# Adding the residual in one-tile transfers, with a larger descriptor room and other buffer addresses, in a hybrid conv/RWKV decoder layer

## The chip, the cores and the metric

The kernel runs on one core of a Trainium2 chip. A core has TensorE (PE, matmuls into PSUM), VectorE (DVE), ScalarE (ACT), GpSimd (POOL), and SyncE (SP), which here only issues transfers between DRAM and the on-chip SBUF; sixteen DMA engines carry them. GpSimd issues transfers too, through a queue of its own whose descriptors stand in a piece of SBUF that the program sets aside. The metric is device microseconds for the whole layer, median of several runs; lower is better.

## What is computed

One decoder layer over 512 positions and 16 learned meta tokens ahead of them, model width 2048, all float32:

```python
n = rmsnorm(h, g_pre_mix)
z = n @ w_in                                   # 2048 -> 6592 columns
y_conv = short_conv_group(z[..., :CONV_COLS], conv_w)
y_rwkv = rwkv7_group(z[..., CONV_COLS:], ...)  # token shift, low-rank gates, a scan over 16 heads of 64
mix = jnp.concatenate([y_conv, y_rwkv], axis=-1) @ w_out
h = h + rmsnorm(mix, g_post_mix)               # the residual addition that the change touches
f = conv_glu(rmsnorm(h, g_pre_ffn), w_gate_up, conv_ffn, w_down)   # 2048 -> 2 x 5632 -> 2048
h = h + rmsnorm(f, g_post_ffn)
```

## The kernel before

Activations lie transposed: 16 k tiles of 128 channels (partitions) by positions. Every large product is made of three float32r products of a rounded part and a remainder (hi·hi, hi·lo, lo·hi): ScalarE rounds (`S.copy`, or an activation with a scale), VectorE subtracts to get the remainder. For weights, a raw tile of 512 KB comes into one of five buffers R; `parted` (L1313) rounds it into H or another tile and puts the remainder in O or another tile.

The first stage (about 0 to 760 us) computes the input projection, the RWKV scan and the convolution group. Its pool of tiles, p1, is given back and a second pool, p2, takes the memory. Then `w_out` is multiplied, into `acc` (in this part called `h`), for two halves of the positions: columns 0 to 257 (half 0) and 258 to 513 (half 1).

Then comes the part around the change. `rms1(i)` (L1245) makes the reciprocal root `r1[i]` of half i from the sums of squares. `residual(i)` (L1271) goes through the k tiles in eight pairs: VectorE multiplies the pair by `r1`, GpSimd issues a transfer that reads the layer's input `xT` from DRAM and adds it into the tile in SBUF (`accum_op=ALU.add`), and then `split` scales, rounds and takes the remainder of each of the two tiles: these are the moving operands of the feed-forward's first products, `tt` (block `b11`) for k tiles 0 to 7 of half 0, and `ahi`/`alo` for the others. In half 1 SyncE also stores the pair, 512 KB, to DRAM (`hsp`), and ScalarE and VectorE square and sum the tiles for the next norm (`beside`, L1547).

TensorE meanwhile runs `halves2` (L1530) for the first two column blocks of the feed-forward, f = 0 and f = 1: all of half 0 for both, then half 1. Each k tile of a half feeds 12 matmuls of 128x128 by 256 or 258 columns: gate and up of two blocks, three products each. f = 2 and 3 follow, and then a long, regular stretch of sevenfold products to the end.

Everything up to the first units of that stretch is recorded first and put in order by a planner (class `Plan`): `run` (L423) lets a model of the five engines walk through the recorded work, with a cost for each instruction (`time`, 0.9 us for a GpSimd transfer) and a time of landing (`land`, L330: bytes at 230 GB/s, one transfer behind the other, and a fixed part), eight times with new ranks; the best order is written out, and every engine executes its list in that order. A late transfer therefore also holds up whatever stands behind its reader.

GpSimd's issues stand in its list one after the other, with one square sum of the norm among the first. A helper records every operation, so that nearly all instructions of the profile carry its line, L223; tiles tell them apart.

Of the kernel before, what the change touches and what calls it, by code (L numbers as in the profile page):

```python
# [10 lines left out]
F32 = mybir.dt.float32  # L11
F32R = mybir.dt.float32r
AF = mybir.ActivationFunctionType
ALU = mybir.AluOpType
# [8 lines left out]
KT = D // 128  # L23
CW = 1024
NP = 8
# [3 lines left out]
T0 = META - 2  # L29
TY = L - T0  # L30
# [9 lines left out]
COLS = {}  # L40
NCOL = 0
# [50 lines left out]

FILL = 9

TRIES = 8
LAND, GAP = 1.2, {"PE": 0.3, "DVE": 0, "ACT": 0, "POOL": 0, "SP": 0}

# [25 lines left out]
class View:  # L123
# [57 lines left out]
        return self.then("unsqueeze", (d,), {}, self.parts, np.expand_dims(self.ids, d))  # L181

    def to_broadcast(self, shape):
        return self.then("to_broadcast", (shape,), {}, self.parts, self.ids)

    def bitcast(self, dtype):
        return self.then("bitcast", (dtype,), {}, self.parts, self.ids)
# [39 lines left out]
class Plan:  # L227
# [195 lines left out]
    def run(self, rank):  # L423

        units, cost = self.units, self.cost
        left, ready = [len(b) for b in self.before], [0.0] * len(units)
        wait, go = {e: [] for e in HOP}, {e: [] for e in HOP}
        free, busy = dict.fromkeys(HOP, 0.0), dict.fromkeys(HOP, (0.0, False))
        free["PE"] = self.head
        self.pipe, table, kind = 0.0, 0, (128, 128)  # L430
        began, ends = [0.0] * len(units), [0.0] * len(units)
        for u in range(len(units)):
            if not left[u]:
                heapq.heappush(wait[self.engine[u]], (0.0, u))
        for _ in units:
            t, e = min((free[e] if go[e] else max(free[e], wait[e][0][0]), i, e) for i, e in enumerate(HOP)
                       if go[e] or wait[e])[::2]
            while wait[e] and wait[e][0][0] <= t:
                u = heapq.heappop(wait[e])[1]
                heapq.heappush(go[e], (rank[u], u))  # L440
            u = heapq.heappop(go[e])[1]
            x = units[u][0]
            start = t
            if e in ("DVE", "POOL") and self.two(x):
                end, two = busy["POOL" if e == "DVE" else "DVE"]
                if two and end > t:

                    aside = [u]
                    while e == "DVE" and go[e] and self.two(units[aside[-1]][0]):
                        aside.append(heapq.heappop(go[e])[1])  # L450
                    u = aside.pop() if not self.two(units[aside[-1]][0]) else aside.pop(0)
                    for v in aside:
                        heapq.heappush(go[e], (rank[v], v))
                    x = units[u][0]
                    if self.two(x):
                        start = end
            d = cost[u]
            if e == "ACT":
                k = self.TABLE.get(x["kw"].get("func"), 0)
                if k and k != table:  # L460
                    d, table = d + 1.28, k
            if e == "PE":
                k = self.mode(x)
                if k != kind:
                    d, kind = d + (0.25 if k == (128, 128) else 0.1), k
            began[u], ends[u] = t, start + d
            free[e], busy[e] = start + d, (start + d, self.two(x))
            dma = x["op"] == "dma_start"
            end = self.land(x, start + d) if dma else start + d + (0.22 if e == "PE" else 0)
            for v in self.after[u]:  # L470
                o = self.engine[v]
                ready[v] = max(ready[v], start + d if o == e and not dma else end + 0.07 + GAP[o])
                left[v] -= 1
                if not left[v]:
                    heapq.heappush(wait[o], (ready[v], v))
        return began, ends
# [13 lines left out]
def hymba(tc, I, out, ysp=None):  # L490
    nc = tc.nc
# [6 lines left out]
    def pool(ctx, name, bufs, kind="sbuf"):  # L498
        kw = {} if kind == "sbuf" else {"space": PSUM if kind == "psum" else DRAM}
        return Pool(plan, ctx.enter_context(tc.tile_pool(name=name, bufs=bufs, **kw)), bufs, kind)  # L500

    cp, ap, wp = pool(ctx, "cp", 1), pool(ctx, "ap", 1), pool(ctx, "wp", 2)
    mp, dp = pool(ctx, "mp", 2, "psum"), pool(ctx, "dp", 1, "dram")
    plan.on = True

    par = cp.tile([128, NCOL], F32, name="par")
    SP.dma_start(par[:, :KT], I["par"][:, :KT])
    ones = cp.tile([128, 128], F32, name="ones")
    z0 = cp.tile([128, 1], F32, name="z0")
    V.memset(z0, 0.0)  # L510
    S.activation(out=z0, in_=z0, func=AF.Copy, scale=1.0)
    omu = cp.tile([128, 28 + NP], F32, name="omu")

    def pc(n, i):
        return par[:, COLS[n] + i:COLS[n] + i + 1]

    if ysp is None:
        ysp = dp.tile([KT, 128, TY], F32, name="ysp")
# [64 lines left out]
    def rms(ss, r, m, q, psp, tag, pb=2, eps=None, o=None):  # L583


        n = r.shape[-1]
        ps = psp.tile([128, 512], F32, name="psn", tag=tag, bufs=pb)[:, :n]
        for i, x in enumerate(ss):
            PE.matmul(ps, ones, x, start=(i == 0), stop=(i == len(ss) - 1))
        if eps is None:  # L590
            V.tensor_scalar(out=m, in0=ps, scalar1=1.0 / D, scalar2=EPS, op0=ALU.mult, op1=ALU.add)
        else:
            V.scalar_tensor_tensor(out=m, in0=ps, scalar=1.0 / D, in1=eps, op0=ALU.mult, op1=ALU.add)
        rsqrt_guess(m, r, q)
        V.tensor_scalar(out=q, in0=q, scalar1=-0.5, scalar2=1.5, op0=ALU.mult, op1=ALU.add)
        V.tensor_tensor(out=r if o is None else o, in0=r, in1=q, op=ALU.mult)
# [4 lines left out]

    with ExitStack() as ctx1:
        p1, aux, stp = pool(ctx1, "p1", 1), pool(ctx1, "aux", 2, "psum"), pool(ctx1, "st", 2, "psum")
        cst = p1.tile([128, 64 + 9 * C], F32, name="cst")
        gmask = cst[:, :64]
        smask = cst[:, 64:]
        SUV = []
        for i in range(3):
            t = p1.tile([128, 2, 2, 64], F32, name=f"SUV{i}")
# [9 lines left out]
        for k in range(KT):  # L619
            xr = p1.tile([128, LP], F32, name="krv"[k % 3], bufs=2)[:, :L]  # L620
            SP.dma_start(xr, I["xT"][k])
            if k == 1:
                SP.dma_start(par[:, KT:], I["par"][:, KT:])
                V.tensor_scalar(out=omu[:, :28], in0=par[:, COLS["mu"]:COLS["mu"] + 28], scalar1=-1.0, scalar2=1.0,
                                op0=ALU.mult, op1=ALU.add)
                V.tensor_scalar(out=omu[:, 28:], in0=par[:, COLS["k_a"]:COLS["k_a"] + NP], scalar1=-1.0, scalar2=1.0,
                                op0=ALU.mult, op1=ALU.add)
            if k == 2:
                SP.dma_start(ones, I["cst"][:, :128])
                SP.dma_start(cst, I["cst"][:, 256:])  # L630
            if k == 0:
                first = wload(I["w_in"][0][0])
            hi, lo = a_tiles(k, L)
            split(xr, hi, lo, pc("g_pre", k))
            xs.append((hi, lo))
            sq = p1.tile([128, LP], F32, name=("sg", "al", "t1", "t2", "t3", "Pi")[k if k < 2 else 2 + k % 4])[:, :L]
            S.activation(out=sq, in_=xr, func=AF.Square)
            if k < 2:
                ss.append(sq)
            else:  # L640
                (G, V)[k % 2].tensor_tensor(out=ss[k % 2], in0=ss[k % 2], in1=sq, op=ALU.add)
# [576 lines left out]
    with ExitStack() as ctx2:  # L1218
# [16 lines left out]
        def big(tag, dtype=F32R):  # L1235
            return p2.tile([128, 1024], dtype, name=tag, bufs=WB[tag])
# [34 lines left out]
        def residual(i):  # L1271

            a, b = HY[i]
            c, d = WIN[i]
            for m in range(0, KT, 2):
                x, src = h[:, m:m + 2, a:b], I["xT"][m:m + 2, :, T0 + a:T0 + b].rearrange("m p t -> p m t")
                V.tensor_tensor(out=x, in0=x, in1=r1[i].unsqueeze(1).to_broadcast([128, 2, b - a]), op=ALU.mult)
                G.dma_start(x, src, accum_op=ALU.add)
                for n in (m, m + 1):
                    with plan.step(1):  # L1280
                        split(h[:, n, c:d], *act(n, i), pc("g_ffn", n))
                if i:
                    SP.dma_start(hsp[m:m + 2].rearrange("m p t -> p m t"), h[:, m:m + 2, 2:])
                yield
# [46 lines left out]

        def sums(j):

            y = [big("R", F32)[:, :TY] for _ in range(2)]
            for x, k in zip(y, (j, H + j)):
                SP.dma_start(x, ysp[KORD[k]])
            t = two()
            less(t[:, 0], y[1][:, 256:], y[0][:, 256:])
            plus(t[:, 1], t[:, 0], y[0][:, :258])
            x = y[1][:, :258]  # L1340
            less(x, x, t[:, 1])
            for o, x in ((T2, t[:, 1]), (T3, t[:, 0]), (T4, x)):
                split(x, o[:, j, 0], o[:, j, 1])
# [660 lines left out]
```

## Time and profile before

| | |
|---|---|
| median of 3 runs | 2448.86 us (2447.86 to 2452.65) |
| the profiled execution | 2448.97 us, span 2447.2 us |
| TensorE busy | 2375.2 us, 97% of the span |
| VectorE, ScalarE, GpSimd busy | 1755.9, 1228.2, 647.5 us |
| mean DMA rate | 113 GB/s |
| mean granted TensorE clock | 0.985 |

Three stretches are not full of matmuls: the first microseconds, where the first tiles are loaded; about 960 to 1062 us, the part described above; and the last 28 us. A row of the timeline has the start, the time, the engine, the operation with its output and inputs, a count, and in brackets the idle time before it with what ended it. "issue" there means that the profile shows no wait that the engine had. A group's row has its total and mean time, and the idle time before its members.

### The profile page before, as it was taken

To read this page: it belongs to the slowest core of one execution; us is meant where nothing else is said; L and a number is where in the kernel's file an instruction comes from. 1 tells how busy PE (TensorE), PEld (TensorE's weight loads), DVE (VectorE), ACT (ScalarE), POOL (GpSimd) and SP (SyncE) were. 2 spreads that over 40 slices of the span, in tenths; PEclk is the share of its full clock that TensorE was granted. 3 is DMA by queue.
4 is the path that set the end of the run, shared out by engine and by line. 5 is a ranking of instruction groups with operands and counts; after the bars stand their busy time and mean duration, and the time that the engine had idled before them with its cause. 6 is when DMAs were issued, how large, how long until landed. Compare 5 with 4: busy or idle time off the path is not lost.

```text
span 2447.2 us, 46249 instructions
## 1 busy us (share of the span) xinstructions
PE 2375.2 (97%) x18450; PEld 2253.0 (92%) x18450; DVE 1755.9 (72%) x2361; ACT 1228.2 (50%) x2404; POOL 647.5 (26%) x742
## 2 busy tenths in 40 slices
PE   7999999999999999599999999999999999999996
PEld 7999999999999999499999999898989898989896
DVE  7678888879745776267676767686868585959586
ACT  7766766767654555265443434342435252525254
POOL 2222646465450022201121212121212020202025
PEclk9999999999999999699999999999999999999998
DMA  5444333333434745533232324242424242323352
GB/s 179 150 130 118 93 84 92 105 105 94 127 105 132 231 136 178 107 94 97 85 121 79 121 78 129 69 131 69 134 74 130 78 120 85 111 91 102 98 193 71
DMA packets 136295, 276.82 MB, mean 113 GB/s; under 512 B 30576, under 2 KB 47728, under 8 KB 136080
## 3 DMA queue, kind: packets, MB, share of 16 engines
q1 hardware_dynamic: 131728, 269.66, 36.1%
q0 software_dynamic: 4352, 4.21, 1.3%
q8 instruction: 145, 2.38, 0.4%
q14 instruction: 70, 0.57, 0.1%
HBM read 247.99 MB, written 25.84 MB: 112 GB/s over the span
## 4 chain that ended last, share of the span: by engine, by line
PE 89%; issue 3%; DVE 3%; DMA 2%; ACT 2%; POOL 1%; SPq 0%; ACTq 0%; POOLq 0%; DVEq 0%
PE mps L223 56%; PE u L223 17%; PE d L223 10%; PE st L223 4%; PE aux L223 2%; DVE acc L223 1%; POOL acc L223 1%; DMA acc<-xT_dram 0%; DMA R<-w_down_dram 0%; DMA l<-lo 0%; DVE raw L223 0%; DMA k<-xT_dram 0%; DMA d<-tb 0%; DVE O L223 0%; DVE alo L223 0%
## 5 line engine op out<-in xcount | busy, mean ns | idle before, releaser
L223 ACT CAST H<-R 128x1024 fp32r<-128x1024 f32 x401 | 419.2, 1047 | 492.7 <-PE u L223 187.0
L223 DVE TENSOR_TENSOR O<-R,H 128x1024 fp32r<-128x1024 f32 x401 | 521.9, 1302 | 126.6 <-ACT H L223 119.5
L223 PE MATMUL mps<-ahi,whi 128*128 128x264 f32 (+2 forms) x1824 | 365.1, 289 | 10.6 <-ACT whi L223 10.6
L223 PE MATMUL mps<-alo,whi 128*128 128x264 f32 (+2 forms) x1824 | 364.3, 289 | 0.9 <-DVE alo L223 0.9
L223 PE MATMUL mps<-ahi,wlo 128*128 128x264 f32 (+2 forms) x1824 | 361.5, 288 | 1.6 <-DVE wlo L223 1.6
L223 PE MATMUL mps<-tt,H 128*128 128x258 f32 x2160 | 290.2, 284 | 7.5 <-ACT tt L223 6.2
L223 PEld LDWEIGHTS mps<-ahi,whi 128*128 128x128 f32 x1824 | 278.6, 189 | 13.2 <-ACT whi L223 10.8
L223 PE MATMUL mps<-ahi,H 128*128 128x258 f32 x1064 | 262.8, 287 | 25.9 <-ACT ahi L223 25.5
L223 PEld LDWEIGHTS mps<-tt,H 128*128 128x128 f32 x2160 | 273.5, 190 | 10.5 <-ACT tt L223 7.2
L223 DVE TENSOR_TENSOR wlo<-raw,whi 128x512 fp32r<-128x512 f32 x261 | 198.6, 765 | 117.8 <-ACT whi L223 102.4
L223 PEld LDWEIGHTS mps<-alo,whi 128*128 128x128 f32 x1824 | 278.0, 189 | 3.5 <-DVE alo L223 1.1
L223 PEld LDWEIGHTS mps<-ahi,wlo 128*128 128x128 f32 x1824 | 277.5, 190 | 3.8 <-DVE wlo L223 1.8
L223 POOL TENSOR_TENSOR raw<-raw,rb 128x516 f32<-128x516 f32 (+1 forms) x45 | 91.5, 2034 | 677.0 <-DVE raw L223 628.0
L223 PE MATMUL mps<-alo,H 128*128 128x258 f32 x1064 | 263.1, 287 | 0.4
L223 POOL TENSOR_TENSOR R<-R 128x1024 f32<-128x1024 f32 x40 | 131.7, 3292 | 429.6 <-DVE R L223 429.6
L223 DVE TENSOR_TENSOR R<-R 128x1024 f32<-128x1024 f32 x136 | 227.7, 1674 | 1.6 <-DMA R<-w_pair_dram 0.3
L223 PEld LDWEIGHTS mps<-ahi,H 128*128 128x128 f32 x1064 | 200.4, 191 | 28.9 <-ACT ahi L223 28.4
L223 ACT CAST whi<-raw 128x512 fp32r<-128x512 f32 x261 | 160.2, 618 | 119.0 <-PE mps L223 74.0
L223 PEld LDWEIGHTS mps<-alo,H 128*128 128x128 f32 x1064 | 201.8, 193 | 2.9 <-DVE alo L223 2.9
L223 POOL TENSOR_SCALAR SUV<-VT 32x64 f32<-32x64 f32 x272 | 138.7, 510 | 159.6 <-PE st L223 132.8
L223 PE MATMUL mps<-ahi,O 128*128 128x258 f32 x1064 | 159.9, 286 | 0.0
L223 PE MATMUL mps<-tt,O 128*128 128x258 f32 x1080 | 153.6, 281 | 0.0
(323 smaller groups left out, 4603.6 us busy)
## 6 DMA issues: line engine op xcount, KB each, us to landing
R<-w_gu_dram SPq DMA_DIRECT2D x176, 512.0 KB, 3.6
raw<-w_in_dram SPq DMA_DIRECT2D x208, 256.0 KB, 2.7
R<-w_down_dram SPq DMA_DIRECT2D x88, 512.0 KB, 3.7
raw<-w_out_dram SPq DMA_DIRECT2D x32, 256.0 KB, 4.4
R<-w_pair_dram SPq DMA_DIRECT2D x16, 512.0 KB, 4.5
l<-lo SPq DMA_DIRECT2D x24, 264.0 KB, 2.3
R<-ysp SPq DMA_DIRECT2D x16, 257.0 KB, 4.3
hsp<-acc SPq DMA_DIRECT2D x8, 512.0 KB, 2.8
```

The source lines that it names most:

```text
L223: return getattr(self.real, op)(*real, **{k: x.get() if isinstance(x, View) else x for k, x in kw.items()})
```

## The change

- The room for GpSimd's descriptors goes from 1024 to 2048 bytes per partition (`DGE`).
- `residual` issues a transfer for each k tile, two for a pair, where it issued one; the product on VectorE and the stores stay in pairs.
- The planner gets a list `ring` of GpSimd's transfers in flight: one of 128 partitions counts 2 + 128 // 8 = 18 entries, `DGE // 16` = 128 entries are there, and a transfer that finds no room waits for the earliest landing.
- The room comes out of SBUF: `ones` becomes one column, set by VectorE and read as a repeated column (it was loaded, 64 KB), and the parameters are kept in two tiles, of which the one for the first stage, and `omu`, lie in p1. `to_broadcast` now also repeats the numbers by which dependences are found.
- In `sums` the two rows for j = 0 go to H and O instead of two R buffers. The pool places tiles in the order of their first use, so H and O now lie at 150784 to 175359 bytes of each partition (before: 200416 to 224991), and the three blocks `tt` behind them (175360 to 224895; before 150880 to 200415). Most other tiles move by 96 bytes.

```diff
+DGE = 2048
...
+                n = 2 + x["out"].parts // 8
+                while sum(k for t, k in ring if t > start) + n > DGE // 16:
+                    start = min(t for t, _ in ring if t > start)
...
-            end = self.land(x, start + d) if dma else start + d + (0.22 if e == "PE" else 0)
+            if dma and e == "POOL":
+                ring.append((self.land(x, start + d), n))
+            end = ring[-1][0] if dma and e == "POOL" else self.land(x, start + d) if dma else start + d + (0.22 if e == "PE" else 0)
...
-    par = cp.tile([128, NCOL], F32, name="par")
-    SP.dma_start(par[:, :KT], I["par"][:, :KT])
-    ones = cp.tile([128, 128], F32, name="ones")
+    NMIX = COLS["g_post"]
+    par = [None, cp.tile([128, NCOL - NMIX], F32, name="par")]
+    ones = cp.tile([128, 1], F32, name="ones")
...
-            PE.matmul(ps, ones, x, start=(i == 0), stop=(i == len(ss) - 1))
+            PE.matmul(ps, ones.to_broadcast([128, 128]), x, start=(i == 0), stop=(i == len(ss) - 1))
...
-                SP.dma_start(ones, I["cst"][:, :128])
+                V.memset(ones, 1.0)
                 SP.dma_start(cst, I["cst"][:, 256:])
+                SP.dma_start(par[1], I["par"][:, NMIX:])
...
-                x, src = h[:, m:m + 2, a:b], I["xT"][m:m + 2, :, T0 + a:T0 + b].rearrange("m p t -> p m t")
+                x, src = h[:, m:m + 2, a:b], I["xT"][m:m + 2, :, T0 + a:T0 + b]
                 V.tensor_tensor(out=x, in0=x, in1=r1[i].unsqueeze(1).to_broadcast([128, 2, b - a]), op=ALU.mult)
-                G.dma_start(x, src, accum_op=ALU.add)
+                for n in range(2):
+                    G.dma_start(x[:, n], src[n], accum_op=ALU.add)
...
-            y = [big("R", F32)[:, :TY] for _ in range(2)]
+            y = [big(n, F32)[:, :TY] for n in ("RR" if j else "HO")]
...
-    nc = bacc.Bacc("TRN2", target_bir_lowering=False, num_devices=1, dynamic_dma_scratch_size=1024)
+    nc = bacc.Bacc("TRN2", target_bir_lowering=False, num_devices=1, dynamic_dma_scratch_size=DGE)
```

GpSimd's list from the last square sums on, before. "waits" names whose signals the instruction waits for; DMASW0 to 7 are eight counters that GpSimd's transfers use in turn.

```order
L223 TENSOR_TENSOR hxh<-hxh,q 128x258 [waits Activation_49,Pool_49]
L223 DMA acc<-xT_dram 128x2x258 [waits DVE_49] x2
L223 TENSOR_TENSOR hxh<-hxh,q 128x256 [waits Activation_49,Pool_49]
L223 DMA acc<-xT_dram 128x2x258 [waits DVE_49] x6
L223 DMA acc<-xT_dram 128x2x256 [waits DMASW0_49,DVE_49]
L223 DMA acc<-xT_dram 128x2x256 [waits DMASW1_49,DVE_49]
```

And now:

```order
L226 TENSOR_TENSOR hxh<-hxh,q 128x258 [waits Activation_49,Pool_49]
L226 DMA acc<-xT_dram 128x258 [waits DVE_49]
L226 DMA acc<-xT_dram 128x258
L226 DMA acc<-xT_dram 128x258 [waits DVE_49]
L226 TENSOR_TENSOR hxh<-hxh,q 128x256 [waits Activation_49,Pool_49]
L226 DMA acc<-xT_dram 128x258
L226 DMA acc<-xT_dram 128x258 [waits DVE_49]
L226 DMA acc<-xT_dram 128x258
L226 DMA acc<-xT_dram 128x258 [waits DVE_49]
L226 DMA acc<-xT_dram 128x258
L226 DMA acc<-xT_dram 128x258 [waits DMASW0_49,DVE_49]
L226 DMA acc<-xT_dram 128x258 [waits DMASW1_49]
```

Each transfer moves half as much, the square sum stands behind the third instead of the second, and from the ninth transfer on each waits for the landing of the one eight places earlier; before, that began with the ninth pair.

ScalarE's list where the last tiles of half 1 are rounded (`ahi`), with the squares (`q<-acc`) and the first rounding of the weights of f = 2 (`H<-R`), before:

```order
L223 ACTIVATE ahi_13820<-acc,par 128x258
L223 ACTIVATE raw<-acc 128x514
L223 ACTIVATE q<-acc 128x514 [waits DVE_49] x3
L223 ACTIVATE ahi_13827<-acc,par 128x258 [waits DMASW6_49]
L223 ACTIVATE ahi_13837<-acc,par 128x258
L223 ACTIVATE q<-acc 128x514 [waits DVE_49] x2
L223 CAST H<-R 128x1024 [waits PE_49]
L223 ACTIVATE ahi_13872<-acc,par 128x258 [waits DMASW7_49]
L223 ACTIVATE ahi_13878<-acc,par 128x258
```

And now:

```order
L226 ACTIVATE ahi_13854<-acc,par 128x258 [waits DMASW0_49]
L226 ACTIVATE q<-acc 128x514 [waits DVE_49] x2
L226 CAST H<-R 128x1024 [waits PE_49]
L226 ACTIVATE ahi_13866<-acc,par 128x258 [waits DMASW1_49]
L226 ACTIVATE ahi_13901<-acc,par 128x258 [waits DMASW2_49]
L226 ACTIVATE q<-acc 128x514 [waits DVE_49] x2
L226 CAST H<-R 128x1024 [waits DMAHW4_49,PE_49]
L226 ACTIVATE ahi_13907<-acc,par 128x258 [waits DMASW3_49]
L226 ACTIVATE ahi_13918<-acc,par 128x258 [waits DMASW4_49]
```

Every rounding now waits for its own tile's transfer, and two weight roundings, which wait for TensorE, stand ahead of five or more of the last tiles where one stood ahead of two.

More of the change, by code (lines that the diff above doesn't have):

```diff
@@ L183, in to_broadcast @@
     def to_broadcast(self, shape):
-        return self.then("to_broadcast", (shape,), {}, self.parts, self.ids)
+        ids = np.broadcast_to(self.ids, (len(self.ids),) + tuple(shape[1:]))
+        return self.then("to_broadcast", (shape,), {}, self.parts, ids)
     def bitcast(self, dtype):
@@ L429, in run @@
         free["PE"] = self.head
+        ring = []
         self.pipe, table, kind = 0.0, 0, (128, 128)
@@ L457, in run @@
             d = cost[u]
+            if e == "POOL" and x["op"] == "dma_start":
+                n = 2 + x["out"].parts // 8
+                while sum(k for t, k in ring if t > start) + n > DGE // 16:
+                    start = min(t for t, _ in ring if t > start)
             if e == "ACT":
@@ L511, in hymba @@
     S.activation(out=z0, in_=z0, func=AF.Copy, scale=1.0)
-    omu = cp.tile([128, 28 + NP], F32, name="omu")
     def pc(n, i):
-        return par[:, COLS[n] + i:COLS[n] + i + 1]
+        c = COLS[n] + i
+        return par[0][:, c:c + 1] if c < NMIX else par[1][:, c - NMIX:c - NMIX + 1]
     if ysp is None:
@@ L603, in hymba @@
         p1, aux, stp = pool(ctx1, "p1", 1), pool(ctx1, "aux", 2, "psum"), pool(ctx1, "st", 2, "psum")
+        par[0] = p1.tile([128, NMIX], F32, name="parm")
+        SP.dma_start(par[0][:, :KT], I["par"][:, :KT])
+        omu = p1.tile([128, 28 + NP], F32, name="omu")
         cst = p1.tile([128, 64 + 9 * C], F32, name="cst")
@@ L622, in hymba @@
             if k == 1:
-                SP.dma_start(par[:, KT:], I["par"][:, KT:])
-                V.tensor_scalar(out=omu[:, :28], in0=par[:, COLS["mu"]:COLS["mu"] + 28], scalar1=-1.0, scalar2=1.0,
+                SP.dma_start(par[0][:, KT:], I["par"][:, KT:NMIX])
+                V.tensor_scalar(out=omu[:, :28], in0=par[0][:, COLS["mu"]:COLS["mu"] + 28], scalar1=-1.0, scalar2=1.0,
                                 op0=ALU.mult, op1=ALU.add)
-                V.tensor_scalar(out=omu[:, 28:], in0=par[:, COLS["k_a"]:COLS["k_a"] + NP], scalar1=-1.0, scalar2=1.0,
+                V.tensor_scalar(out=omu[:, 28:], in0=par[0][:, COLS["k_a"]:COLS["k_a"] + NP], scalar1=-1.0, scalar2=1.0,
                                 op0=ALU.mult, op1=ALU.add)
             if k == 2:
-                SP.dma_start(ones, I["cst"][:, :128])
+                V.memset(ones, 1.0)
                 SP.dma_start(cst, I["cst"][:, 256:])
+                SP.dma_start(par[1], I["par"][:, NMIX:])
             if k == 0:
```

## The prediction

> **What bounds the kernel now.** I read the page's slices first. TensorE is at nine tenths or more nearly everywhere; inside the kernel only slices 16 and 17 (61.2 us each) fall off, and the granted clock falls with them.
>
> ```profile
> PE   7999999999999999599999999999999999999996
> PEclk9999999999999999699999999999999999999998
> ```
>
> Next the busy time by stretch. Columns: stretch, its length, busy us and count of TensorE, its weight loads, VectorE, ScalarE and GpSimd, then clock, DMA share and GB/s.
>
> ```profile
> 1080.00:1100.00 20.00, 20.00 (x168) 20.00 (x168) 15.71 (x27) 16.71 (x33) 1.31 (x1) 1.00 0.19 54
> 972.67:1062.64 89.97, 57.37 (x299) 50.39 (x299) 34.43 (x63) 29.13 (x57) 17.05 (x14) 0.70 0.55 116
> 1062.64:1074.10 11.46, 11.46 (x98) 11.46 (x98) 7.16 (x13) 4.73 (x11) 1.29 (x1) 1.00 0.47 134
> ```
>
> The norm's four float32 sums (8 records), and the row behind them, from TensorE's timeline:
>
> ```profile
> 1060.74 1.90 PE L223 MATMUL psn<-raw,ones 128*128 128x258 f32 x8
> 1062.29 0.47 PE L223 MATMUL mps<-tt,H 128*128 128x258 f32 x1
> ```
>
> An undisturbed 20 us holds 168 matmuls, 0.119 us each. From 972.67, where the first feed-forward matmul starts, to 1074.10, where the work of the feed-forward's first two column blocks would be done, there are 299 + 98 = 397 records. At 0.119 us they need 47.2 us; the sums (1.55 us from start to start for 8 records, instead of 0.95) make it 47.9. The stretch took 101.4 us, so 53.5 us are lost here, in idling and at half clock. The timelines of VectorE, GpSimd and then ScalarE say what paces it.
>
> ```profile
> 963.77 4.90 DVE L223 TENSOR_TENSOR acc<-acc,r1p 128x516 f32<-128x516 f32 x8
> ...
> 964.78 1.39 POOL L223 DMA_DIRECT2D acc<-xT_dram  x1 [5.47 <-DVE acc L223]
> 969.63 1.23 POOL L223 DMA_DIRECT2D acc<-xT_dram  x1 [3.46 <-ACT acc L223]
> 975.46 1.20 POOL L223 DMA_DIRECT2D acc<-xT_dram  x1 [3.93 <-issue]
> 980.34 1.24 POOL L223 DMA_DIRECT2D acc<-xT_dram  x1 [3.68 <-issue]
> 985.30 1.21 POOL L223 DMA_DIRECT2D acc<-xT_dram  x1 [3.72 <-issue]
> 1044.97 1.22 POOL L223 DMA_DIRECT2D acc<-xT_dram  x1 [5.29 <-issue]
> ```
> ```profile
> 975.22 0.91 ACT L223 ACTIVATE tt<-acc,par 128x258 fp32r<-128x258 f32 x2 [2.21 <-DMA acc<-xT_dram]
> 980.04 0.91 ACT L223 ACTIVATE tt<-acc,par 128x258 fp32r<-128x258 f32 x2 [3.09 <-DMA acc<-xT_dram]
> 985.01 0.91 ACT L223 ACTIVATE tt<-acc,par 128x258 fp32r<-128x258 f32 x2 [4.05 <-DMA acc<-xT_dram]
> 1051.44 0.91 ACT L223 ACTIVATE ahi<-acc,par 128x258 fp32r<-128x258 f32 x2 [3.87 <-DMA acc<-xT_dram]
> ```
>
> The pair issued at 975.46 has landed at 980.04, and the next is issued at 980.34, 0.3 us later; 985.01 and 985.30 repeat it. So one pair is in flight at a time, and each cycle is 1.22 us of issue, 3.36 us of flight and 0.3 us. VectorE's eight products of the first half are there at 968.7, so "issue", the profile's word for no wait that it can see, is here a wait for the former transfer. That fits a full descriptor store: by the change's own rule a tile takes 2 + 128/8 = 18 of the room's entries, 1024/16 = 64 of them, and a pair, having twice the runs, at least 34. Two pairs do not fit. TensorE stands behind every landing, and below it ScalarE and VectorE wait in the same rhythm:
>
> ```profile
> 985.57 1.10 PE L223 MATMUL mps<-tt,H 128*128 128x258 f32 x2 [3.22 <-ACT tt L223]
> 1052.00 0.58 PE L223 MATMUL mps<-ahi,H 128*128 128x258 f32 x1 [2.84 <-ACT ahi L223]
> L223 ACT ACTIVATE ahi<-acc,par 128x258 fp32r<-128x258 f32 x24 | 10.9, 503 | 48.5 <-DMA acc<-xT_dram 48.5
> L223 DVE SCALAR_TENSOR_TENSOR alo<-acc,par,ahi 128x258 fp32r<-128x258 f32 x24 | 10.6, 486 | 44.9 <-ACT ahi L223 44.9
> ```
>
> **The transfers, and their room.** Sixteen transfers of a pair become 32 of a tile, and 128 entries hold seven of 18. Three things can now set the pace.
>
> *GpSimd's issue.* A one-tile issue is not in the trace. Its bounds are 0.61 us (half of 1.22, all by descriptors) and 1.22 us (all fixed); I take 1.2, since a small fixed part cannot be read from one size. 32 issues from 964.78, with the square sum that stands after the third (1.13 us in the group rows),
>
> ```profile
> L223 POOL TENSOR_TENSOR hxh<-hxh,q 128x256 f32<-128x256 f32 x1 | 1.1, 1130 | 0.0
> L223 POOL DMA_DIRECT2D acc<-xT_dram x16 | 19.7, 1229 | 66.5 <-issue 54.2 <-DVE acc L223 8.9 <-ACT acc L223 3.5
> ```
>
> end at 964.78 + 39 + 1.1 = 1005; with a full pair's flight behind, the last tile is there at 1008 (at 0.61 us it would be 989). The new waits in the order, each for the transfer eight places earlier, are met: eight issues take 9.6 us, issue and flight 4.6.
>
> *The DMA engines.* One pair alone kept them busy 0.41 of 5.00 us, 2.05 us, so 1.03 us a tile:
>
> ```profile
> 980.30:985.30 5.00, 1.60 (x9) 1.20 (x9) 0.89 (x2) 0.95 (x3) 1.24 (x1) 0.77 0.41 53
> q1 hardware_dynamic: 131728, 269.66, 36.1%
> ```
>
> That is the upper bound. The lower is the rate of the other queue, 269.66 MB in 36.1% of 2447.2 us, 305 GB/s, or 0.43 us a tile. The same engines carry the eight 512 KB stores of the sum (1.7 us each at 305 GB/s) and weights: 0.55 of 89.97 us, 49.5 us of work, all in the stretch. If nothing overlaps better, that ends at 972.67 + 49.5 = 1022; the last store and two weight loads (5 us) may come after the last tile, so this tile lands by 1017 at the latest. Between 1005 and 1017 I expect 1010.
>
> *TensorE.* 972.67 + 47.9 = 1020.6. A tile feeds 12 matmuls, 1.43 us, which is slower than 1.2 us of issue. Behind the last tile lie one rounding (0.50), one remainder (0.49) and 12 matmuls: 1017 + 2.4 = 1019.4 still comes first. So with perfect order TensorE becomes its own bound, and the gain is at most 53.5 us.
>
> What comes off: ScalarE and VectorE take their work in order. VectorE has 34.4 + 7.2 = 41.6 us in the two stretches, to be done in about 50; the sums of squares now stand between the splits, and two weight roundings on ScalarE wait for TensorE between the last tiles. The order itself counts 0.9 us for each issue, where I count 1.2, so the last tiles come up to 32 x 0.3 = 10 us later than it thinks. TensorE's slower appetite covers part of that. Bounds are 0 and 20 us: 10 by the order, the rest where a stall costs the clock. How that goes is seen behind the row at 1052.00 (columns here: stretch, length, TensorE, clock, DMA share, GB/s): 17 matmuls in 4 us at clock 0.50, then 34 in 4.9 us. 51 took 8.9 us instead of 6.1, so the gap cost 2.8 us more.
>
> ```profile
> 1052.00:1056.00 4.00, 4.00 (x17) 0.50 0.35 133
> 1056.00:1060.90 4.90, 4.90 (x34) 0.78 0.10 7
> ```
>
> [...]
>
> I take 8.5 us, somewhat under the middle. Gain: 53.5 - 8.5 = 45.
>
> **The rest, at nothing.** H and O move, and so do the three blocks tt and nearly every other tile. Rows of unlike addresses show the same durations: the remainder written to tt or to O, and matmuls from whi or from H.
>
> ```profile
> L223 DVE TENSOR_TENSOR tt<-R,tt 128x1024 fp32r<-128x1024 f32 x4 | 4.8, 1217 | 0.0
> L223 DVE TENSOR_TENSOR O<-R,H 128x1024 fp32r<-128x1024 f32 x2 | 2.4, 1220 | 0.0
> L223 PE MATMUL mps<-ahi,whi 128*128 128x264 f32 (+2 forms) x1824 | 365.1, 289 | 10.6 <-ACT whi L223 10.6
> L223 PE MATMUL mps<-ahi,H 128*128 128x258 f32 x1064 | 262.8, 287 | 25.9 <-ACT ahi L223 25.5
> ```
>
> Loading j = 0 of the mixer's sums into H and O, the memory that other tiles give up late, and the reordered first stage all lie under a full TensorE:
>
> ```profile
> 800.00:820.00 20.00, 20.00 (x167) 19.95 (x167) 12.00 (x19) 9.42 (x20) 0.00 (x0) 1.00 0.68 200
> 300.00:400.00 100.00, 99.05 (x929) 94.06 (x928) 83.39 (x154) 65.73 (x191) 57.05 (x105) 1.00 0.33 93
> ```
>
> Uncovered, a planner's other choice costs or wins about what such 100 us lose, 1 us; I allow 2 either way. At the start the 64 KB of ones and 90 KB of parameters leave the front of the queue: at 305 GB/s 0.5 us less at the most, where TensorE's first wait of 10.03 us hangs on loads. The weight of ones is now read from one column; if those loads took twice their 0.19 us, the 17 sums would lose 6 us, and 0 if a repeated column is read like any other. I take 0, as the same number of columns goes in.
>
> ```profile
> 10.03 0.81 PE L223 MATMUL mps<-ahi,whi 128*128 128x264 f32 x2 [10.03 <-ACT whi L223]
> ...
> L223 PEld LDWEIGHTS psn<-raw,ones 128*128 128x128 f32 x7 | 1.3, 189 | 0.1
> ```
>
> **Sum.** The profiled execution took 2448.97 us, 0.1 over the median of 2448.86 and 1.8 over its own span:
>
> ```profile
> span 2447.2 us, 46249 instructions
> ```
>
> What lies around the span stays. 2448.97 - 45 = 2404 us.
>
> **Rivals.**
>
> *One in flight still, so slower.* If it is not the room but the accumulating transfer itself that goes one at a time, 32 cycles stand where 16 stood. A cycle would be 0.61 to 1.22 of issue, 1.68 to 3.36 of flight, and 0.3: 2.6 to 4.9 us. The 16 took 1051.44 - 964.78 = 86.7 us, so from 2.71 us a cycle on the change loses. At the middle, 3.75 us, it is 120 us: 33 more, 2482 us. For it: the 0.3 us between landing and issue looks the same either way. Against: the same numbers follow from 64 entries without any further rule. 7%.
>
> [...]
>
> *Delivery stays the bound.* If fewer than seven fit, or the stores crowd the reads more than 49.5 us says, a tile comes every 1.9 us, say: last landing 964.78 + 61 + 3.4 = 1029 instead of 1051.4, with as much behind it as now. Gain 22, 2427 us; the pace decides from about 1.5 us a tile. For it: from issue to landing it is already 5.1 us beside the stores, in the second half, against 4.6. 15%.
>
> ```profile
> acc<-xT_dram POOLq DMA_DIRECT2D x8, 258.0 KB, 4.6
> ...
> acc<-xT_dram POOLq DMA_DIRECT2D x8, 256.0 KB, 5.1
> ```
>
> *The change does not free the room* (the store keeps its size, tiles half as large go two at a time, or less): a cycle near 2.7 us per tile and no change, 2449. 3%.
>
> **Numbers.** Forecast, with its own range 2395 to 2416: 70%. Below it (a better start or order): 5%. Delivery-bound, 2416 to 2438: 15%. No change 3%, slower 7%. The range 2395 to 2430 takes in the forecast and most of the second rival and leaves out under 2 in 10. Less than 0.2% (5 us) cannot be told from none here: faster 0.90, same 0.03, slower 0.07.
>
> **What would show it.** Right: GpSimd's transfers start about 1.2 us apart with no 3.5 us of "issue" between; the last rounding of a residual tile near 1010; TensorE dense from 973 at clock 1.00, and later stages the same but 45 us earlier. Issue to landing may grow. Wrong: starts 2.5 us apart or more (the room was not it); dense transfers but TensorE idle behind VectorE or ScalarE (order); a longer mean of the remainder or the matmuls after 1130 (addresses); other gaps before 960.

## The result, and the profile after

The changed kernel takes 2384.24 us (median of 5 runs, 2380.68 to 2385.08), the kernel before, on the same chip, 2448.35 (2447.04 to 2452.65): a ratio of 0.9732, with a 95% interval of 0.9718 to 0.9746. That is 64 us less, where 45 were forecast, and below the range of 2395 to 2430. Direction and the mechanism of the residual stretch were right; two terms of the sum were not. One execution of a later kernel (the line for H and O alone), at a mean granted clock of 0.556, took 3829.02 us; it is left out of that kernel's time. The profiled execution took 2381.91 us with a span of 2380.1, against 2447.2, so between the two traces 67.1 us have to be accounted for.

The slices of the profile after, TensorE and its clock. The dip of slices 16 and 17 is gone:

```profile
PE   7999999999999999999999999999999999999996
PEclk9999999999999999999999999999999999999998
```

A record is one instruction in the trace. The 393 starts of TensorE (393 to 397 records, by how the ends of a window cut them) that took from 972.67 to 1074.08 before now run from 972.84 to 1021.36. The row of that stretch (columns as in the prediction: busy us and count of TensorE, its weight loads, VectorE, ScalarE, GpSimd, then clock, DMA share, GB/s):

```profile
972.84:1021.36 48.52, 48.41 (x396) 47.89 (x395) 37.51 (x74) 32.65 (x66) 23.10 (x26) 1.00 0.96 239
```

It lasts 48.5 us where it lasted 101.4, TensorE is busy in all of it, and the clock is 1.00, where the first 90 us before had 0.70. The prediction's floor for it was 47.9. The DMA engines are now at 0.96, where those 90 us had 0.55.

GpSimd's timeline, then the groups that showed the old rhythm:

```profile
965.43 2.82 POOL L226 DMA_DIRECT2D acc<-xT_dram  x3 [5.48 <-DVE acc L226]
967.92 1.01 POOL L226 TENSOR_TENSOR hxh<-hxh,q 128x256 f32<-128x256 f32 x1
968.50 10.21 POOL L226 DMA_DIRECT2D acc<-xT_dram  x11
979.56 1.76 POOL L226 DMA_DIRECT2D acc<-xT_dram  x2 [0.85 <-DMA acc<-xT_dram]
981.50 0.86 POOL L226 DMA_DIRECT2D acc<-xT_dram  x1 [0.17 <-issue]
...
987.81 8.94 POOL L226 DMA_DIRECT2D acc<-xT_dram  x10 [0.40 <-issue]
```
```profile
L226 POOL DMA_DIRECT2D acc<-xT_dram x32 | 29.0, 1491 | 7.6 <-DVE acc L226 5.5 <-DMA acc<-xT_dram 0.9 <-issue 0.6
...
L226 ACT ACTIVATE ahi<-acc,par 128x258 fp32r<-128x258 f32 x24 | 11.7, 506 | 6.2 <-DMA acc<-xT_dram 6.2
...
L226 DVE SCALAR_TENSOR_TENSOR alo<-acc,par,ahi 128x258 fp32r<-128x258 f32 x24 | 10.9, 485 | 3.4 <-ACT ahi L226 3.4
```

Eleven transfers go out in one row of 10.21 us, 0.93 us each; a single one takes 0.86 (issues overlap in the trace, so that the group's mean of 1491 ns is longer than this pace). The last has been issued at 996.75 (987.81 + 8.94): 32 in 31.3 us, 0.98 us a tile. "issue" shrank from 54.2 us to 0.6, ScalarE's wait for landings from 48.5 to 6.2, VectorE's behind it from 44.9 to 3.4. Counted transfer by transfer, from issue to landing, at most one pair was under way before and at most seven tiles are now. The last rounding of a tile starts at 1007.36. What grew is the time from issue to landing, from 4.6 and 5.1 us for a pair in the two halves to 6.6 and 7.1 for a tile, with more under way at once (KB each, median us):

```profile
hsp<-acc SPq DMA_DIRECT2D x8, 512.0 KB, 6.5
...
acc<-xT_dram POOLq DMA_DIRECT2D x16, 129.0 KB, 6.6
...
acc<-xT_dram POOLq DMA_DIRECT2D x16, 128.0 KB, 7.1
```

The stretch accounts for 52.9 us, less 0.2 by which it starts later. The other 14.4 come behind it, and evenly: matmul by matmul, the distance between the two traces stays at 52.7 us from the end of the stretch to record 9500 (1077 us of the profile after) and then grows by about 1.4 us in each of the ten rounds of sevenfold products and `w_down`, to 67.1. Waiting is not the reason: between records 9500 and 18000 TensorE idled 0.3 us before, and not at all now, and its matmuls come in the same order. It is the matmuls themselves. Rows of the kernel before, and then after, by groups of one shape:

```profile
L223 PE MATMUL u<-whi,H 128*128 128x512 f32 x240 | 94.6, 394 | 0.0
...
L223 PE MATMUL u<-hxh,H 128*128 128x512 f32 x80 | 31.5, 394 | 0.0
...
L223 PE MATMUL u<-hxl,H 128*128 128x512 f32 x80 | 31.5, 394 | 0.0
```
```profile
L226 PE MATMUL u<-whi,H 128*128 128x512 f32 x240 | 93.5, 390 | 0.0
...
L226 PE MATMUL u<-hxl,H 128*128 128x512 f32 x80 | 31.6, 395 | 0.0
...
L226 PE MATMUL u<-hxh,H 128*128 128x512 f32 x80 | 31.1, 389 | 0.0
```

These are the products of `w_down`: the hidden activations `whi`, `wlo`, `hxh`, `hxl` move, 512 columns of them, over weights in H and O. A record's length, 389 to 395 ns here, is longer than the time from its start to the next one, so the starts tell more. From start to start a 512-wide matmul took 232.4 ns before and takes 227.4 now (1920 of them, 446.2 and 436.5 us: 9.7 us); those from `hxl` alone went up, from 232.3 to 234.2. The 258-wide ones of the same stretch went from 120.5 to 119.8 ns (some 6840, 4.9 us). A `w_down` block of 192 matmuls lasts 43.7 us instead of 44.6, and in 40 us of it there are 178 records instead of 174 (before, after):

```profile
1645.00:1685.00 40.00, 40.00 (x174) 32.35 (x173) 22.82 (x27) 8.18 (x9) 0.66 (x1) 1.00 0.22 67
```
```profile
1586.00:1626.00 40.00, 40.00 (x178) 33.03 (x177) 23.61 (x28) 8.34 (x10) 1.43 (x1) 1.00 0.22 67
```

So there were two questions. Which part of the change freed the residual stretch, the room or the smaller transfers? And what makes a matmul faster whose instruction, order and waits are unchanged?

### The profile page after: what moved, and what is told of

It is laid out like the page before. It is cut to its first block, busy times and chain, and to the rows that moved or that the text cites. A ratio compares the mean times of both kernels' runs of the same rounds, so it can differ in the third digit from the quotient of the medians.

```text
span 2380.1 us, 46315 instructions
## 1 busy us (share of the span) xinstructions
PE 2340.4 (98%) x18450; PEld 2233.7 (94%) x18450; DVE 1753.1 (74%) x2362; ACT 1229.2 (52%) x2404; POOL 651.6 (27%) x758
## 4 chain that ended last, share of the span: by engine, by line
PE 92%; DVE 3%; DMA 2%; issue 1%; ACT 1%; SPq 1%; POOL 0%; DVEq 0%; ACTq 0%; POOLq 0%
PE mps L226 58%; PE u L226 18%; PE d L226 10%; PE st L226 4%; PE aux L226 2%; DVE acc L226 1%; SPq L226 1%; DMA R<-w_down_dram 0%; DMA raw<-w_in_dram 0%; DVE alo L226 0%; DMA ysp<-sg 0%; DMA d<-tb 0%; PE psn L226 0%; DVE O L226 0%; DVE q L226 0%
## 5 line engine op out<-in xcount | busy, mean ns | idle before, releaser
L226 DVE TENSOR_TENSOR O<-R,H 128x1024 fp32r<-128x1024 f32 x401 | 522.3, 1303 | 119.9 <-ACT H L226 110.7
L226 PE MATMUL mps<-alo,H 128*128 128x258 f32 x1064 | 257.9, 283 | 0.0
L226 PE MATMUL mps<-ahi,H 128*128 128x258 f32 x1064 | 257.8, 282 | 0.0
L226 DVE TENSOR_TENSOR R<-R 128x1024 f32<-128x1024 f32 x136 | 226.8, 1668 | 2.2 <-DMA R<-w_pair_dram 0.9
```

The lines of the kernel that those rows point to most:

```text
L226: return getattr(self.real, op)(*real, **{k: x.get() if isinstance(x, View) else x for k, x in kw.items()})
```

## Experiments on the addresses

Four theories stood for the 14 us. *Region*: memory from 196608 bytes on is slower to read, and H and O have left it. *Moving address*: a moving operand is read faster from a multiple of 256 bytes (`whi` went from 76896 to 76800). *Weight address*: the same for the weights (H went from 224 over a multiple of 256 to 0). *Traffic*: addresses matter only against what other engines read and write. The runs led to a fifth.

**Second row of addresses.** The line for H and O undone, the rest of the change kept:

```diff
-            y = [big(n, F32)[:, :TY] for n in ("RR" if j else "HO")]
+            y = [big(n, F32)[:, :TY] for n in "RR"]
```

> The changed kernel with both rows of sums in R buffers again, so that H and O go back up to 200320 to 224895 bytes, now at 128 over a multiple of 256; whi, wlo and hxh keep their multiples of 256. Region and weight-address theory: 512-wide matmuls at 232 ns from start to start again, so the 14 us of the sevenfold stretch are lost: 2398 us. Moving-address theory: 227 ns stay, 2384 us (hxl at 234 as now). If H and O have nothing to do with it at all, 2384 too.

2400.21 us, a ratio of 0.9791 (0.9777 to 0.9806) against the 0.9732 of the change. 512-wide matmuls are at 232.4 ns again, and 40 us of `w_down` hold 173:

```profile
1597.00:1637.00 40.00, 40.00 (x173) 32.34 (x173) 23.04 (x28) 7.97 (x8) 0.96 (x1) 1.00 0.21 66
```

The residual stretch takes 48.6 us as after the change. So the two gains are separate, the 14 us belong to that one line, and the moving address by itself falls: `whi` still stands at a multiple of 256.

**All tiles shifted by 96 bytes**, H and O left low:

```diff
-    ones = cp.tile([128, 1], F32, name="ones")
+    ones = cp.tile([128, 25], F32, name="ones")[:, :1]
```

> The changed kernel with 96 bytes left empty ahead of the activations: every tile from ahi on lies 96 bytes higher, as before the change (whi, wlo and hxh at 96, hxl at 224 over a multiple of 256, H and O at 96), but H and O stay low, at 150880 to 175455. Region theory: 2384 us, 227 ns. Moving-address theory: 232 ns, 2394 to 2398 us. Weight-address theory: the same 232 ns, 2394 to 2398 us.

2383.85 us, 0.9731 (0.9714 to 0.9747), 226 to 227 ns (`hxl` 234.2). No multiple of 256 is left, neither of moving operand nor weights, and nothing is lost: the weight address falls too, and region seems to hold.

**The line for H and O alone**, in the kernel before:

> The kernel before with the one line of the change that puts the rows of j = 0 into H and O: pairs, the small room and the load of ones stay, H and O lie at 150880 to 175455, whi, wlo and hxh at 96 over a multiple of 256 as before. Region theory: 512-wide matmuls at 227 ns, 2448.4 - 14.4 = 2434 us. Moving-address and weight-address theory (neither stands at a multiple of 256): 232 ns, 2448 us. On every theory the residual stretch keeps its one transfer in flight and its 53.5 us.

2438.94 us, 0.9951 (0.9934 to 0.9968), and 226 to 227 ns (`hxl` 234.2): 12 us of gain with pairs, small room and all. In the traces 13.6 us are won from record 9500 on, and 3.5 lost ahead of it. Region forecast 2434, the others no change.

**Only matmuls.** This kernel leaves the whole layer out; groups of 12 matmuls run over one piece of x with no other engine at work:

```python
for w in (wa, wb, wc, wd):      # 75264, 79584, 197120, 201440: 0, 224, 0, 224 over a multiple of 256
    for m in low + high:        # 8 from 83712 on, 8 from 205568 on: 0, 32, ... 224 over a multiple of 256
        for i in range(3):      # 36 matmuls
            ps = group(w, m, n, i % 2)
```

> This kernel leaves the whole layer out: it only multiplies one 512 KB piece of x, in groups of 12 matmuls as w_down's products have them (weights 128x128 from two places 2 KB apart, moving operand 128x512, then 128x258), with no other engine at work. The weights stand in four places, low or high (75264 and 197120 bytes of a partition) and at an address that is 0 or 224 over a multiple of 256; the moving operand in sixteen, low or high, at 0, 32, ... 224 over a multiple of 256. 36 matmuls for each of the 64 combinations. Region theory (what lies at 196608 bytes or more is slower to read): about 227 ns from start to start for 512 columns where both are low, 232 where one is high, whatever the remainder. Moving-address theory: 227 where the moving operand starts at a multiple of 256, 232 to 234 elsewhere, whatever the weights. Weight-address theory: 227 for the two weights at a multiple of 256, 232 for the other two. Traffic theory (addresses matter only against the other engines' reads and writes): all 64 alike within 1 ns.

All four theories failed. Start to start, 512 columns, ns; the distance is the moving operand's address minus that of the weights, modulo 256:

```
distance             0      32     64     96    128    160    192    224
weights  75264   227.3   233.4  229.1  233.7  233.4  234.2  233.3  233.2
weights  79584   227.4   233.4  229.2  233.7  233.4  234.2  233.3  233.2
weights 197120   227.4   233.4  229.1  233.7  233.4  234.2  233.3  233.1
weights 201440   227.4   233.4  229.2  233.7  233.4  234.2  233.3  233.2
```

Rows for low and high moving operands agree within 0.2 ns and stand as one (the very first combination is left out: its first 13 matmuls started some 427 ns apart, nearly twice the pace behind them). Neither region nor either address decides, only their distance. Six groups of that profile show it in the lengths (`ha` lies at 0 over a multiple of 256, `hh` and `lh` at 224, all but `lh` above 196608; `wa`, `wc` at 0, `wb`, `wd` at 224):

```profile
L48 PE MATMUL ps<-ha,wb 128*128 128x512 f32 x36 | 8.6, 395 | 0.0
...
L48 PE MATMUL ps<-hh,wa 128*128 128x512 f32 x36 | 8.6, 395 | 0.0
...
L48 PE MATMUL ps<-hh,wd 128*128 128x512 f32 x36 | 8.4, 390 | 0.0
...
L48 PE MATMUL ps<-ha,wc 128*128 128x512 f32 x36 | 8.3, 390 | 0.0
...
L48 PE MATMUL ps<-ha,wa 128*128 128x512 f32 x36 | 8.3, 390 | 0.0
...
L48 PE MATMUL ps<-lh,wb 128*128 128x512 f32 x36 | 8.3, 390 | 0.0
```

This is the *distance* theory, and it reads the layer's runs so far: `whi` to H is 123520 bytes before, 128 modulo 256, and 73984 after, 0 modulo 256. The shift by 96 bytes moved both and kept 0; the second row of addresses made it 128 again. Region had fitted three runs by chance, since H went low and to distance 0 at once.

**The distances in finer steps:**

```python
for n, step, span in ((512, 4, 256), (258, 2, 128), (264, 8, 128)):   # in float32s
    for o in range(0, span, step):
        for _ in range(3):
            group(o, n, lambda k: (w, o))
for a, b in ((64, 96), (96, 64), (64, 64), (96, 96)):
    for _ in range(4):
        group(0, 512, lambda k: ((w, a), (v, b))[k % 2])
```

> Again only matmuls of one piece of x, the layer left out. One pair of weights, all its slices at a multiple of 512 bytes, and a moving operand whose start goes through 64 distances from the weights: 0 to 1008 bytes in steps of 16 for 512 columns, 0 to 504 in steps of 8 for 258, in steps of 32 for 264; 36 matmuls each. At the end 512 columns with weights that alternate between two tiles (w at 0, v at 128 over a multiple of 512) and moving operands at 256 and 384, so that either a matmul's own weights, or those of the next matmul (which are loaded while it runs), lie 256 away. Distance theory (what counts is moving address minus weight address, modulo 512): 227 ns at 256 and 768, 233 at 128 and 384, 229 at 64 over 256, the same in both halves of the 1024 bytes; at 0 the 232 of hxl before the change. Had the remainder by 256 been enough, 0 and 512 would also take 227. If the own weights count, the first order of the last part takes 227 and the second 233; if the next ones count (their load runs beside the matmul), the other way round. Region and traffic theories: one pace for all.

```
bytes        0     16     32     48     64     80     96    112
512 wide  226.7  231.5  233.4  233.2  229.2  230.9  233.6  231.1
bytes      128    144    160    176    192    208    224    240
512 wide  232.4  233.0  234.2  233.3  233.1  234.5  233.2  226.9
```

The row repeats with a period of 256, within 0.2 ns and with 227.7 or 227.8 at 256, 512 and 768. So 256 and not 512 is the modulus, against what I had taken from `hxl`. At 258 columns the pace lies between 117.2 ns (at 16) and 122.7 (at 104), at 264 between 120.0 (at 0) and 126.5 (at 96). The part on whose weights count settled nothing: with weights in turn from w and v, 228.4 ns where a matmul's own weights lie at distance 0 and the next one's at 128, 230.0 where it is the other way round, and 232.3 and 232.1 in the two controls that mix both. A matmul's pace is then not a sum of its own distance and its neighbour's; this stays open.

**128 bytes, and nothing else.** In the kernel before, tt2 made longer:

```diff
-            return p2.tile([128, H, 2, 258], F32R, name=f"tt{n}", bufs=1)
+            x = p2.tile([128, 2 * H * 258 + (32 if n == 2 else 0)], F32R, name=f"tt{n}", bufs=1)
+            return x[:, :2 * H * 258].rearrange("p (h q t) -> p h q t", h=H, q=2)
```

> The kernel before with tt2 128 bytes longer, so that H, O, hxl and rb move up by 128 bytes and nothing else: H at 200544, O at 212832, all above 196608 still; whi, wlo and hxh lie 256 modulo 512 from them (before 128), hxl 0 as before. Distance theory: 512-wide matmuls at 227 ns from whi, wlo and hxh, 232 from hxl, and 2448 - 13 = 2435 us. Region theory: 232 ns and 2448 us. The residual stretch as before in both.

2438.04 us, 0.9944 (0.9929 to 0.9959): 14 us for 128 unused bytes, with H and O still above 196608, and with the same instructions in the same order on every engine. All 512-wide matmuls are at 226.5 to 227.0 ns by groups, and 40 us of `w_down` hold 178, where they held 174 before:

```profile
1643.00:1683.00 40.00, 40.00 (x178) 33.14 (x177) 23.44 (x28) 8.55 (x9) 1.26 (x1) 1.00 0.23 70
```

The matmuls at 227 ns include those of `hxl`, for which I had expected 232: its distance is 0 and was 0 before, when it took 232.3 between neighbours at 128. So here too a matmul's own distance is not the whole story. The same 128 bytes in the kernel of the second row of addresses, whose instructions and order they leave as they are:

> The second experiment's kernel (rows of sums in R, H and O above 200 KB) with tt2 128 bytes longer: H at 200448, O at 212736, hxl at 225024, whi, wlo and hxh where they were, so that all distances between 512-wide moving operands and their weights are 0 modulo 256. Every instruction and its place in the order is the second experiment's. Distance theory: all 512-wide matmuls at 227 ns, also those from hxl, 2400 - 14 - 1 = 2385 us. If the second experiment had lost its time by the lower place of the tt blocks, the reads in the sums or the order: still 2400.

2380.70 us, 0.9715 (0.9701 to 0.9728), against 2400.21 us and 0.9791; 178 matmuls in 40 us of `w_down` instead of 173. Between the same two records of the sevenfold stretch the traces differ by 16.5 us. Another 5 us lie in the first stage, where neither order nor addresses differ. Differences of this size occur there without one in the program: between the changed kernel and the one of the next experiment, whose first stages are the same too, it is 4.6 us.

**Only `hxl` moved**, in the changed kernel, by the same longer tt2:

> The changed kernel with tt2 128 bytes longer, which moves only hxl and rb: hxl then lies 0 modulo 256 from H and O (128 with the change). Distance theory: the 160 matmuls from hxl at 227 ns where they took 234, 160 x 7.5 ns = 1.2 us: 2383, too little to be told by the times. Else 234 and 2384.

Its matmuls go from 234.2 to 226.8 ns, their groups from 395 to 389:

```profile
L226 PE MATMUL u<-hxl,H 128*128 128x512 f32 x80 | 31.1, 389 | 0.0
```

The time is 2383.61 us, 0.9723 (0.9710 to 0.9736), and the changed kernel itself, on the same chip:

> The changed kernel itself, for a comparison on the same chip: 0.9732 of the kernel before, 2384 us.

2383.48 us, 0.9729 (0.9716 to 0.9743). The 1.2 us cannot be seen in the times, and the high H and O with the right distance (0.9715) are not shown to be faster than the change either; their intervals overlap.

## Experiments on the transfers

**Pairs with the large room:**

```diff
-                for n in range(2):
-                    G.dma_start(x[:, n], src[n], accum_op=ALU.add)
+                G.dma_start(x, src, accum_op=ALU.add)
...
-                n = 2 + x["out"].parts // 8
+                n = 2 + 2 * x["out"].parts // 8
```

> The changed kernel with a pair for each transfer again and the room of 2048 bytes (the planner counts a pair as 34 entries of 128, three in flight). Room theory: GpSimd issues pairs 1.2 to 2 us apart with no 3.5 us between, the last lands by 1005, TensorE stays full: 2384 us, within 5. Size theory (a pair goes alone whatever the room): one each 5 us, the 53.5 us are back, 2437.

2388.26 us, 0.9745 (0.9728 to 0.9761). The room alone brings nearly everything: the stretch takes 50.4 us against 48.5, at full clock.

```profile
975.73:1026.11 50.38, 49.68 (x393) 48.26 (x394) 37.83 (x72) 31.79 (x66) 14.69 (x13) 1.00 0.94 227
```

GpSimd's "issue" falls to 6.7 us, and its last pair has been issued at 1005.15, 37.2 us after the first:

```profile
L226 POOL DMA_DIRECT2D acc<-xT_dram x16 | 19.7, 1314 | 22.0 <-issue 6.7 <-DVE acc L226 5.5 <-DVE r1p L226 3.2
```

**Single tiles with the small room:** `DGE = 1024`, which the planner also takes for its list.

> The changed kernel with the small room of 1024 bytes, 64 entries, in which three tiles of 18 fit, and the planner told so; all other tiles lie 1024 bytes lower, so the distances stay. Room theory: three in flight, each there some 3 to 4.6 us after its issue begins: 1.0 to 1.5 us a tile, the last landing between 997 and 1013, before TensorE is done: 2384 to 2390 us. If a transfer into the accumulating path went alone in the small room whatever its size: 32 x 2.6 to 4.9 us, 2450 to 2500. Size theory (smaller transfers alone cure it): 2384.

2397.56 us, 0.9778 (0.9763 to 0.9792): 13 us behind the change, more than the room theory's 2384 to 2390. In the profiled execution it is 18 us, of which the stretch, with 58.5 us, has 10 and the first stage 7, which these runs do not explain. The groups of GpSimd and ScalarE, and two of the waits on TensorE:

```profile
L226 POOL DMA_DIRECT2D acc<-xT_dram x32 | 28.3, 935 | 26.0 <-issue 15.3 <-DVE acc L226 5.2 <-DVE r1p L226 2.7
...
L226 ACT ACTIVATE ahi<-acc,par 128x258 fp32r<-128x258 f32 x24 | 12.2, 509 | 20.0 <-DMA acc<-xT_dram 19.8
```
```profile
999.78 0.39 PE L226 MATMUL mps<-ahi,H 128*128 128x258 f32 x1 [1.14 <-ACT ahi L226]
...
1002.61 0.39 PE L226 MATMUL mps<-ahi,H 128*128 128x258 f32 x1 [0.71 <-ACT ahi L226]
```

The 32 issues ran from 973.50 to 1023.93, 1.58 us a tile: just above the 1.5 from which, by the prediction, delivery decides, and TensorE does wait for it. With 4.2 us from issue to landing (3.8 and 4.6 in the two halves) and three in flight, 1.4 were to be had; the rest is GpSimd waiting for products. So both halves of the change help in the same way, by how much is in flight. By the most that the traces show under way at once: one pair (two tiles) before, 101.4 us; three tiles, 58.5; three pairs, 50.4; seven tiles, 48.5.

**The planner kept ignorant of the room:**

```diff
-                n = 2 + x["out"].parts // 8
+                n = 0
```

> The changed kernel, but the planner is not told that the room is bounded (a transfer counts as no entry). It then puts GpSimd's square sum one transfer later and orders some 40 instructions on ScalarE and VectorE and 370 matmuls otherwise. If the room for seven tiles never fills in earnest, as the issues 0.9 us apart say: 2384, within 3 us, TensorE full in the residual stretch. If the order by the bounded room is what made the stalls vanish (I had put them at 8.5 us): some of these come back, 2387 to 2393.

2384.88 us, 0.9729 (0.9715 to 0.9742), the stretch 48.2 us. The list of transfers in flight is worth nothing here, and the freedom from stalls does not come from it.

## Why the prediction was wrong, point by point

**Right: what was lost, why, and where the bound would be.** The 53.5 us of the stretch came back all but 0.6. That a full room keeps one pair in flight, argued from 0.3 us between landing and issue and from the entries of the change's own rule, is shown by the run with pairs in the larger room. The floor of 47.9 us by counted records at 0.119 us met the 48.5 measured, and the estimate of 49.5 us for the DMA engines the 46.6 that they were busy (0.96 of 48.52).

**Harmless: an issue at 1.2 us.** It takes 0.86 to 0.93, so the planner's 0.9 was right, and a pair's 1.22 is, by an estimate from 0.86 and 1.22, some 0.5 fixed and 0.36 a tile. Issues ended at 996.75, not 1005, and the last rounding started at 1007.36, near the 1010 forecast. That nearness is luck: the issues ended 8 us earlier than forecast, but the last tile landed at 1005.92, 9.2 us behind the end of its issue, where 3.4 were assumed. TensorE ended later either way.

**The first step that failed: "I take 8.5 us" for stalls behind late tiles.** No trace shows a term of 8.5, which was my choice between 0 and 20; measured, the stretch took 0.6 us more than its floor. Half of the bound of 20 came from the issue that I had slowed to 1.2 us and the planner had not; with that gone, so was the reason. The other half, a full engine order behind TensorE, met a TensorE that eats a tile in 1.43 us while one comes every 0.98: the last tile was rounded at 1007.9, 13 us before TensorE was done at 1021.4. A term whose bounds were 0 and 20 was put near the middle, though the floor and the delivery times just worked out said the buffer would grow.

**The second step that failed: "The rest, at nothing", for the addresses.** They gave 14.4 us. The rows quoted for it compared matmuls over `whi` and over H by their mean length, 289 and 287 ns, and VectorE's remainders, 1217 and 1220. The second comparison held: over the whole kernel VectorE's 128x1024 remainder into O takes 1303 ns, and took 1302. The first mixed widths (its row of `whi` has 264, 258 and 256 columns) and averaged over many distances, within either row. The 512-wide groups, in which the effect is largest, are not among the quoted rows; but all of them took 232 ns before, so that the trace of before had no row of the faster kind, and the cause could not be read from it. What was open to me was the bound: for an edit that moves operands of TensorE, which was at 97%, 1 ns a matmul over some 8700 matmuls is 9 us, and I allowed 2.

Together the two steps make up the miss: 45 forecast, 7.9 from the first and 14.4 from the second, less the 0.2 by which the stretch starts later, are the 67.1 us between the traces.

**The rest at nothing held.** The stretch starts at 972.84, where it started at 972.67, and the repeated column of ones loads in 188 ns, as the 189 before.

**The rivals.** One in flight still: excluded, since up to three pairs are under way at once in the room for three. Single tiles came every 0.98 us with 6.6 to 7.1 us from issue to landing, so these times were not paid one after the other. Delivery-bound: did not happen, but the small room with single tiles is that case, 10 us worse. That the room does not change: excluded. Below the range had 5%; too little, with one term at a middle between two ends and another at nothing.

## What to carry to other kernels

Where a queue shows "issue" with the same short time between each landing and the next start, as the 0.3 us here, suspect a full room: count what one transfer takes of it, and try a larger room or smaller transfers until delivery is faster than use: here the stretch went from 101.4 us to 50.4 with the one and 58.5 with the other. Where TensorE sets the pace, look at start-to-start times per shape before and after any edit that moves buffers, and try small pads between weights and moving operands: here 128 bytes were worth 14 us of 2452. When a cover is bounded from 0 to something, work out which side is faster before taking a middle.

## What was not expected of the hardware

In these runs the pace of 128x128 float32r matmuls went with the distance of moving operand and weights in SBUF, and repeated every 256 bytes of it. In a row of matmuls with one distance it was, for 512 columns, 226.7 to 227.8 ns at 0, 226.9 at 240, 229.2 at 64, and up to 234.5 (at 208) elsewhere; for 258 columns 117.2 to 122.7. Where distances alternated, the neighbours counted too: `hxl` at 0 took 232.3 ns between neighbours at 128, and 227 between neighbours at 0. The effect was there with no other engine at work, and at one distance the four places of the weights, 75264 to 201440, and low and high moving operands agreed within 0.2 ns. The paces differ by 3% with nothing else changed; by what means the distance enters, the traces here don't show.
